# A hybrid encoder trunk: raw weight loads of the down groups first, three raw buffers, attention bias by transfers

## The chip, the cores and the metric

The kernel runs on one core of one Trainium2 chip. The metric is the device time of one execution in microseconds (us), the median of several runs.

## The reference

Four layers over a sequence of 512 tokens of width 1024, float32. Each layer is a token mixer (convolution module in layers 0 and 3, neighbourhood attention in layer 1, retention in layer 2) and a gated conv-FFN, each with a residual add. The change lies in the FFN and in attention:

```python
def conv_ffn(h, w_up, dw_w, dw_b, w_down):
    u = dwconv(h @ w_up, dw_w, dw_b)          # 1024 -> 2 * 2816, then 3 taps along the tokens
    val, gate = jnp.split(u, 2, axis=-1)
    return (jax.nn.gelu(gate) * val) @ w_down  # 2816 -> 1024

# attention, 16 heads of 64, on a grid of 8 rows x 64 columns
sc = jnp.einsum('bhqd,bhrqwd->bhqrw', q_r, k_win)
sc = sc + bias                                 # from nat_rpb, by relative row and column
p = jax.nn.softmax(sc over the 8 x 16 window)
```

## The kernel before, in words

Every product runs on TensorE in three passes over a high and a low part: a tensor is cast to its high part on ScalarE (ACT), VectorE (DVE) subtracts that from the tensor to get the low part, and `mm3` (L184 to L187) multiplies high by high, low by high, high by low. So each weight tile goes through a raw buffer (`load_raw`, tag `wr`, `NRAW` = 2 of them), a cast (`split_w`, L171) and a difference (L172) into one of three high and three low buffers.

The kernel is a program of tiles. A planner orders the instructions of each engine ahead of time from the order of the program and a timeline of its own; each engine then works through its list strictly in that order. `issue_after` (and `behind`, which looks up a noted instruction) puts an instruction behind another on the same engine's list.

The FFN walks over 22 pairs of columns, value and gate. `up(n)` makes one column of products over the normed input (24 matmuls of 512 tokens); `mid(j)` takes a pair through the three taps (L414, L416, L418), the gelu (L422) and the product (L437). Pairs of pairs make an H pair, `F`, with four blocks and three combinations of them (L444 to L447), split into `Hh` and `Hl`. The first 16 of the 22 pairs (`REST`) are multiplied down by a scheme with seven block products in place of eight, in two groups of four H pairs (`PARTS`); a group starts at the `j` in `starts` and has four macros. Each macro needs a raw weight tile (`r1`, units a11 and a22), a tile `r13` that holds the sums of two pairs of units, and a tile `sg`. `sums` fetches the latter by transfers: a plain one on SP's queue and an accumulating one on GpSimd's (POOL's) queue (L491), then the second plain one on SP's. `weights` loads the raw tile, splits it, splits `r13`, adds the raw tile to it for the third sum (L501, split into h2, l2) and makes the fourth (L505, h4, l4). `prod` multiplies: a11 and a22 first, then s2 (the third sum), s1 and s3 (`r13`), then sg and a12 for the macro before. For a group's first macro the sums are fetched before the mids of that `j`, and `weights` comes after them (`LATEW`); its products with the first three H pairs run ahead of those with the last. The wide intermediates, 128x512, are tiles `t` (`NT_FFN` = 9 buffers in the FFN).

In attention, `proj` projects q, k, v of a group of four heads; q and k are normed with squares and scaling on POOL (L907, L922) and a short chain on VectorE. `att_pair` handles two heads. For each, SP loads a table W of 384 columns (L966) and POOL adds the mask to three windows of it (L970, three adds a head, `NBM` = 2 buffers), with the adds of the first group put behind the squares. `att_step` adds the bias to the scores on VectorE (L995), ScalarE exponentiates, and so on.

Of the kernel before, what the change touches and what calls it, by code (L numbers as in the profile page):

```python
# [8 lines left out]
F32 = mybir.dt.float32  # L9
F32R = mybir.dt.float32r  # L10
# [4 lines left out]
MUL, ADD, SUB = ALU.mult, ALU.add, ALU.subtract  # L15
# [41 lines left out]
NTMP = 3  # L57
NE = 3
NO = 6
NBM = 2  # L60
NORM = "D"
NORDER = "p0 a0 p1 a1 p2 w0 a2 p3 a3 w12 w3".split()
NRAW = 2
HPO = 100000
NQZ = 2
BNG = ((0, 16, 16), (16, 28, 24), (28, 30, 30), (30, 31, 31), (31, 32, 32))
# [5 lines left out]
PART_COL = (0, 2048)  # L72
REST = 16
SLOT_H = 4
NT_FFN = 9
NWS = 3
SCALED = (5, 7, 5, 5)
UPS = ((10, 11, 18, 19), (11, 12, 18, 19), (10, 11, 18, 19), (10, 11, 18, 19))
# [9 lines left out]
def tile_trunk(  # L88
# [17 lines left out]
    def nm(s):  # L106
        uid[0] += 1
        return f"{s}{uid[0]}"
# [85 lines left out]
    def split(src, hi, lo, n=None):  # L194
        state["cast"] = nc.scalar.copy(hi, src)  # L195
        return nc.vector.tensor_tensor(lo, src, hi.bitcast(F32), SUB)  # L196
# [105 lines left out]
    def ffn(l, after):  # L302
        with ExitStack() as st:
# [101 lines left out]
            def mid(j, pv, pg):  # L405
# [41 lines left out]
                nc.vector.scalar_tensor_tensor(F[:, 6, :], F[:, 0, :], -1.0, F[:, 3, :], MUL, SUB)  # L447
                if p + 1 in (p1 for _, p1 in PARTS):
                    for c in (slice(4, 7), slice(0, 1)):
                        split(F[:, c, :], hi[:, c, :], lo[:, c, :])  # L450
                else:
                    split(F, hi, lo)
                H[p] = (hi, lo)
# [26 lines left out]
                    state["spare"] = spare  # L480
                return pss

            def sums(src, gate=None):
                n = src.shape[-1] // 4
                r13 = hp.tile([P, D], F32, tag="ws", name=nm("ws"), bufs=NWS)
                sg = hp.tile([P, D], F32, tag="wq", name=nm("wq"), bufs=2)
                with tc.issue_after(gate.ins) if gate else ExitStack():
                    nc.sync.dma_start(
                        r13[:, :2 * n].rearrange("p (b n) -> p b n", b=2),
                        src[:, 2 * n:3 * n].unsqueeze(1).broadcast_to([P, 2, n]))  # L490
                    nc.gpsimd.dma_start(r13[:, :2 * n], src[:, :2 * n], accum_op=ADD)  # L491
                    nc.sync.dma_start(sg[:, n:2 * n], src[:, 3 * n:])
                return src, r13, sg

            def weights(src, r13, sg):
                n = src.shape[-1] // 4
                r1 = load_raw(src[:, :2 * n], 2 * n)
                w1 = split_w(r1, 2 * n, nc.vector)
                w13 = split_w(r13, 2 * n, nc.vector)
                r2 = r13[:, n:2 * n]  # L500
                nc.vector.tensor_tensor(r2, r2, r1[:, :n], ADD)  # L501
                h2 = hp.tile([P, T], F32R, tag="h2", name=nm("h2"))
                l2 = hp.tile([P, T], F32R, tag="l2", name=nm("l2"))
                split(r2, h2[:, :n], l2[:, :n])
                nc.vector.tensor_tensor(sg[:, :n], r2, sg[:, n:2 * n], ADD)  # L505
                h4 = hp.tile([P, D], F32R, tag="h4", name=nm("h4"))
                l4 = hp.tile([P, D], F32R, tag="l4", name=nm("l4"))
                split(sg[:, :2 * n], h4[:, :2 * n], l4[:, :2 * n])
                u = lambda w, b: (w[0][:, b * n:(b + 1) * n], w[1][:, b * n:(b + 1) * n])
                return {"a11": u(w1, 0), "a22": u(w1, 1), "s3": u(w13, 0), "s1": u(w13, 1),  # L510
                        "s2": u((h2, l2), 0), "sg": u((h4, l4), 0), "a12": u((h4, l4), 1)}

            def down_sums(i, q, gate=None):
                p0, p1 = PARTS[q]
                c = PART_COL[q]
                return sums(f_down[l, i][:, c:c + 4 * (p1 - p0) * P], gate)

            def prod(o, w, q, b, start, stop=True, part=None):
                p0, p1 = PARTS[q]
# [110 lines left out]
            starts = {2 * p1 + (l == 1 and q == 0) * L1 + COVER[q]: q for q, (_, p1) in enumerate(PARTS)}  # L630
            for j in range(1, FT):
                ups_of(j)
                w0 = down_sums(0, starts[j], state["load"]) if j in starts else None
                if w0 and not LATEW:
                    w0 = weights(*w0)
                if n > S2[l]:
                    mids(j)
                if w0 and LATEW:
                    w0 = weights(*w0)
                if w0:  # L640
                    down(starts[j], w0, lambda: mids(j + 1), lambda: ups_of(j + 1))
            mids(FT)
# [217 lines left out]
    def nat(after):  # L860
        PER = 4
        with ExitStack() as st:
            stage_pools(st, NTMP, *NPS)
            np1 = st.enter_context(tc.tile_pool(name=nm("nat"), bufs=1, reuse_waits=RW))
            np2 = st.enter_context(tc.tile_pool(name=nm("nat2"), bufs=2, reuse_waits=RW))
            mask = np1.tile([P, 3, 256], F32, tag="mask", name=nm("mask"))
            nc.scalar.dma_start(mask, nmask.rearrange("p (v k) -> p v k", v=3))
            kstart = (0, 64, 192, 256)
            qzs = [[np1.tile([P, 2, T], F32R, tag=f"qz{n}{i}", name=nm("qz")) for i in range(2)]
                   for n in range(NQZ)]  # L870
# [24 lines left out]
            def proj(g):  # L895
                qk = np2.tile([P, 2, 4, 256], F32, tag="qk", name=nm("qk"), bufs=NQK)
                for part in range(2):
                    pss = part_proj(g, part)
                    with hp():
# [4 lines left out]
                        for t2 in range(2):  # L904
                            sqt = t512()
                            z = qk[:, part, 2 * t2:2 * t2 + 2, :]
                            state["sqt"] = nc.gpsimd.tensor_tensor(  # L907
                                sqt.rearrange("p (t d) -> p t d", t=2), z, z, MUL)
                            nc.vector.tensor_reduce(
                                ss[:, 8 * t2:8 * t2 + 8], sqt.rearrange("p (h d) -> p h d", d=HD),  # L910
                                AX.X, ADD)
# [48 lines left out]
            def att_pair(g, pi, qz, kh, kl, va, vs):  # L960
                hi = np1.tile([P, T], F32R, tag="oh", name=nm("oh"), bufs=NO)
                lo = np1.tile([P, T], F32R, tag="ol", name=nm("ol"), bufs=NO)
                bms = []
                for i2 in range(2):
                    W = np2.tile([P, 384], F32, tag="W", name=nm("W"))
                    nc.sync.dma_start(W, wd[g * PER + pi * 2 + i2])  # L966
                    bm = np1.tile([P, 3, 256], F32, tag="bm", name=nm("bm"), bufs=NBM)
                    for vi, ws in enumerate((128, 64, 0)):
                        with behind("sqt") if g == 0 else ExitStack():
                            nc.gpsimd.tensor_tensor(bm[:, vi, :], W[:, ws:ws + 256],  # L970
                                                    mask[:, vi, :], ADD)
                    bms.append(bm)
                for pr in range(2):
                    for i2 in range(2):
                        r = slice(64 * i2, 64 * i2 + 64)
                        c = slice(pr * 256, pr * 256 + 256)
                        op = att_step(g, pi, i2, pr, qz, kh, kl, bms[i2], va, vs)
                        state["att"] = split(op, hi[r, c], lo[r, c])
                return hi, lo

            def att_step(g, pi, i2, pr, qz, kh, kl, bm, va, vs):
                hh = pi * 2 + i2
# [7 lines left out]
                e = np1.tile([P, T], F32, tag="e", name=nm("e"), bufs=NE)  # L990
                mn, sx, rx = sm(2), sm(2), sm(2)
                for i in range(2):
                    vi = (0, 1, 1, 2)[pr * 2 + i]
                    ei = e[:, i * 256:(i + 1) * 256]
                    nc.vector.tensor_tensor_reduce(  # L995
                        ei, S[:, i * 256:(i + 1) * 256], bm[:, vi, :], -1.0, 3.0e38,
# [389 lines left out]
def _layout(inp):  # L1386
# [44 lines left out]
    for b, ks in ((0, 0), (1, 8), (3, 32)):  # L1431
# [2 lines left out]
        ok = (ks + kc >= start) & (ks + kc < start + 16)  # L1434
        m = np.where(ok, np.float32(0.0), np.float32(-1e30))
        masks.append(np.broadcast_to(m, (16, 8, 32, 8)).reshape(P, 256))
    nmask = np.stack(masks, 1).reshape(P, 768).astype(np.float32)
    rel = (np.arange(DTAB)[None, :] - 384 - np.arange(P)[:, None]).astype(np.float32)

    cdw = np.zeros((2, 64, 16, PH, 5, PH, 16), np.float32)  # L1440
# [71 lines left out]
```

## Time and profile before

| | us |
|---|---|
| median of 3 runs (lowest, highest) | 2544.47 (2542.74, 2549.32) |
| the profiled execution, its own time | 2544.65 |
| its span, first to last instruction | 2542.8 |
| TensorE (PE) busy | 2513.4 |
| VectorE (DVE) busy | 1832.1 |
| ScalarE (ACT) busy | 1266.9 |
| GpSimd (POOL) busy | 389.2 |

The FFNs' first products (L471) start at about 206, 826, 1620 and 2180 us; attention lies between the end of the first FFN and 826. In rows of the profile, `L171 ACT CAST wh<-wr` is a line of the kernel, an engine, an operation and what it writes and reads, with buffer numbers left out; `x` counts instructions; an arrow `<-` behind a time names what ended a wait. A line can be that of a helper, so tiles tell more than lines.

### The profile page before, as it was taken

What the parts mean: (1) busy time and instruction counts of PE and PEld (TensorE: products, weight loads), DVE (VectorE), ACT (ScalarE), POOL (GpSimd) and SP (SyncE); (2) the same over time, 40 slices, a digit from 0 to 9 for tenths busy, and PEclk for the clock granted to TensorE, in tenths of its full rate; (3) what the DMA queues carried; (4) which work ended last, traced back from release to release, by engine and by line L of the source; (5) the groups of instructions that cost most, each with busy time, mean ns of one, the idle gap of its engine ahead of it and who ended that gap; (6) DMA issues with size and microseconds to landing.
All of it is one profiled execution on the core that took longest, in us unless ns stands there. A gap on an engine that the chain in (4) does not pass through costs nothing.

```text
span 2542.8 us, 38763 instructions
## 1 busy us (share of the span) xinstructions
PE 2513.4 (99%) x15166; PEld 2171.4 (85%) x15166; DVE 1832.1 (72%) x3021; ACT 1266.9 (50%) x1778; POOL 389.2 (15%) x475
## 2 busy tenths in 40 slices
PE   9999999999999999999999999999999999999999
PEld 7878798989998889898888888889898887789897
DVE  7986767678877786767666565687677787686765
ACT  5455545465656564555332323464555445464543
POOL 1214010103421201020000000201010121111010
PEclk9999999999999999999999999999999999999999
DMA  7736766744233567673222222476674673477674
GB/s 244 234 97 180 191 154 167 172 135 121 82 92 102 145 171 160 180 185 115 83 76 74 83 75 67 141 185 161 169 169 137 203 224 92 129 195 163 166 164 141
DMA packets 123896, 370.17 MB, mean 146 GB/s; under 512 B 15120, under 2 KB 18064, under 8 KB 123712
## 3 DMA queue, kind: packets, MB, share of 16 engines
q1 hardware_dynamic: 90816, 277.30, 35.1%
q0 software_dynamic: 31600, 87.67, 18.4%
q10 hardware_dynamic: 1296, 2.72, 0.3%
q8 instruction: 119, 1.95, 0.3%
q14 instruction: 65, 0.53, 0.1%
HBM read 333.06 MB, written 30.79 MB: 143 GB/s over the span
## 4 chain that ended last, share of the span: by engine, by line
PE 88%; DVE 4%; DMA 4%; ACT 2%; issue 2%; POOL 0%; DVEq 0%; SPq 0%; ACTq 0%; POOLq 0%
PE ps L185 21%; PE ps L187 21%; PE ps L186 21%; PE ps L315 3%; PE ps L316 3%; PE ps L320 3%; DMA wr<-in_f_down 3%; PE ps L190 3%; PE ps L191 3%; PE ps L192 3%; PE ps L765 1%; DVE wl L172 1%; PE ps L764 1%; PE ps L763 1%; ACT wh L171 1%
## 5 line engine op out<-in xcount | busy, mean ns | idle before, releaser
L171 ACT CAST wh<-wr 128x1024 fp32r<-128x1024 f32 (+1 forms) x311 | 319.1, 1028 | 578.2 <-PE ps L186 280.7
L172 DVE TENSOR_TENSOR wl<-wr,wh 128x1024 fp32r<-128x1024 f32 (+1 forms) x308 | 374.4, 1216 | 197.9 <-ACT wh L171 187.6
L186 PE MATMUL ps<-xl,wh 128*128 128x512 f32 (+1 forms) x1256 | 490.0, 390 | 0.1
L185 PE MATMUL ps<-xh,wh 128*128 128x512 f32 (+1 forms) x1256 | 488.3, 390 | 0.7 <-ACT wh L171 0.7
L187 PE MATMUL ps<-xh,wl 128*128 128x512 f32 (+1 forms) x1256 | 488.6, 390 | 0.1
L185 PEld LDWEIGHTS ps<-xh,wh 128*128 128x128 f32 x1256 | 235.9, 188 | 54.4 <-ACT wh L171 1.6
L186 PEld LDWEIGHTS ps<-xl,wh 128*128 128x128 f32 x1256 | 235.9, 188 | 53.0 <-DVE xl L257 0.5
L187 PEld LDWEIGHTS ps<-xh,wl 128*128 128x128 f32 x1256 | 235.9, 188 | 52.8 <-DVE wl L172 0.5
L185 PE MATMUL ps<-Hh,wh 128*128 128x256 f32 (+1 forms) x734 | 222.5, 310 | 7.4 <-ACT Hh L195 3.7
L186 PE MATMUL ps<-Hl,wh 128*128 128x256 f32 (+1 forms) x734 | 223.8, 308 | 1.4 <-DVE Hl L196 1.4
L187 PE MATMUL ps<-Hh,wl 128*128 128x256 f32 (+1 forms) x734 | 221.9, 308 | 0.5
L315 PE MATMUL ps<-xh,wh 128*128 128x512 f32 x408 | 161.6, 396 | 0.3 <-ACT wh L179 0.3
L316 PE MATMUL ps<-xl,wh 128*128 128x512 f32 x408 | 161.1, 395 | 0.0
L190 PE MATMUL ps<-wh,xh 128*128 128x256 f32 (+1 forms) x512 | 159.0, 313 | 1.2 <-ACT xh L254 1.2
L192 PE MATMUL ps<-wh,xl 128*128 128x256 f32 (+1 forms) x512 | 159.1, 311 | 0.0
L191 PE MATMUL ps<-wl,xh 128*128 128x256 f32 (+1 forms) x512 | 158.9, 311 | 0.0
L185 PEld LDWEIGHTS ps<-Hh,wh 128*128 128x128 f32 x734 | 138.6, 190 | 19.9 <-ACT wh L171 7.3
L186 PEld LDWEIGHTS ps<-Hl,wh 128*128 128x128 f32 x734 | 138.6, 189 | 9.2 <-DVE Hl L196 1.6
L187 PEld LDWEIGHTS ps<-Hh,wl 128*128 128x128 f32 x734 | 137.8, 189 | 9.7 <-DVE wl L172 2.4
L181 POOL DMA_DIRECT2D wl<-in_f_up x51 | 45.0, 883 | 462.0 <-ACT wl L180 271.6
L185 PE MATMUL ps<-Hh,h 128*128 128x256 f32 x384 | 109.4, 285 | 0.6 <-ACT t L546 0.2
L186 PE MATMUL ps<-Hl,h 128*128 128x256 f32 x384 | 108.8, 284 | 0.0
(330 smaller groups left out, 6159.3 us busy)
## 6 DMA issues: line engine op xcount, KB each, us to landing
wr<-in_f_up SPq DMA_DIRECT2D x144, 512.0 KB, 4.1
wraw<-in_cdw SPq DMA_DIRECT2D x56, 608.0 KB, 5.0
wl<-in_f_up POOLq DMA_DIRECT2D x51, 512.0 KB, 7.8
ws<-in_f_down SPq DMA_DIRECT2D x32, 512.0 KB, 7.6
wr<-in_f_down SPq DMA_DIRECT2D x32, 512.0 KB, 7.1
ws<-in_f_down POOLq DMA_DIRECT2D x32, 512.0 KB, 8.4
xd<-t POOLq DMA_DIRECT2D x64, 256.0 KB, 6.7
wr<-in_cw_in SPq DMA_DIRECT2D x30, 512.0 KB, 4.2
```

The lines of the kernel that those rows point to most:

```text
L171: nc.scalar.copy(hi[:, :n], raw[:, :n])
L172: eng.tensor_tensor(lo[:, :n], raw[:, :n], hi[:, :n].bitcast(F32), SUB)
L181: nc.gpsimd.dma_start(lo[:, :n], src.bitcast(F32R), accum_op=ADD)
L185: nc.tensor.matmul(o, wh, ah, start=first, stop=False, skip_group_check=free)
L186: nc.tensor.matmul(o, wh, al, start=False, stop=False, skip_group_check=free)
L187: nc.tensor.matmul(o, wl, ah, start=False, stop=last, skip_group_check=free)
L190: nc.tensor.matmul(o, ah, wh, start=first, stop=False)
L191: nc.tensor.matmul(o, ah, wl, start=False, stop=False)
L192: nc.tensor.matmul(o, al, wh, start=False, stop=last)
L315: nc.tensor.matmul(ps, wh[:, s], xhi[k], start=k == 0, stop=False)
L316: nc.tensor.matmul(ps, wh[:, s], xlo[k], start=False, stop=False)
L320: nc.tensor.matmul(ps, wl[:, k * P:(k + 1) * P], xhi[k], start=False, stop=k == KD - 1)
```

## The change

- `NRAW` 2 to 3 and `NT_FFN` 9 to 7: three raw weight buffers, and in the FFN seven wide intermediates.
- A down group's first macro: its raw tile is loaded in `sums`, behind the last raw load before it, and its sums' transfers on SP come behind that load. The other macros load as before.
- In the same macro, the cast of `r13` is put behind the last Hh cast on ScalarE and its difference behind the last Hl difference on VectorE (`hold`).
- Attention bias: the mask tile, the W tiles and the adds on POOL go. `load_bias` loads the mask straight into a bias tile on SP's queue, and POOL issues a transfer from the table in memory that accumulates the three windows onto it. `NBM` 2 to 4. The masks stand in the reverse order.

```diff
-NBM = 2
+NBM = 4
-NRAW = 2
+NRAW = 3
-NT_FFN = 9
+NT_FFN = 7
...
                     for c in (slice(4, 7), slice(0, 1)):
-                        split(F[:, c, :], hi[:, c, :], lo[:, c, :])
+                        state["Hl"] = split(F[:, c, :], hi[:, c, :], lo[:, c, :])
+                        state["Hh"] = state["cast"]
...
-            def sums(src, gate=None):
+            def sums(src, gate=None, raw=False):
                 n = src.shape[-1] // 4
+                r1 = None
+                if raw:
+                    with tc.issue_after(gate.ins):
+                        r1 = load_raw(src[:, :2 * n], 2 * n)
+                    gate = state["load"]
...
-                return src, r13, sg
+                return src, r13, sg, r1
 
-            def weights(src, r13, sg):
+            def weights(src, r13, sg, r1, hold=False):
                 n = src.shape[-1] // 4
-                r1 = load_raw(src[:, :2 * n], 2 * n)
+                if r1 is None:
+                    r1 = load_raw(src[:, :2 * n], 2 * n)
                 w1 = split_w(r1, 2 * n, nc.vector)
-                w13 = split_w(r13, 2 * n, nc.vector)
+                w13 = (whi.tile([P, D], F32R, tag="wh", name=nm("wh")),
+                       wlo.tile([P, D], F32R, tag="wl", name=nm("wl")))
                 r2 = r13[:, n:2 * n]
+                with behind("Hh") if hold else ExitStack():
+                    nc.scalar.copy(w13[0][:, :2 * n], r13[:, :2 * n])
+                with behind("Hl") if hold else ExitStack():
+                    nc.vector.tensor_tensor(w13[1][:, :2 * n], r13[:, :2 * n],
+                                            w13[0][:, :2 * n].bitcast(F32), SUB)
...
-            def down_sums(i, q, gate=None):
+            def down_sums(i, q):
                 p0, p1 = PARTS[q]
                 c = PART_COL[q]
-                return sums(f_down[l, i][:, c:c + 4 * (p1 - p0) * P], gate)
+                return sums(f_down[l, i][:, c:c + 4 * (p1 - p0) * P], state["load"] if i == 0 else None, i == 0)
...
-                w0 = down_sums(0, starts[j], state["load"]) if j in starts else None
+                w0 = down_sums(0, starts[j]) if j in starts else None
...
                 if w0 and LATEW:
-                    w0 = weights(*w0)
+                    w0 = weights(*w0, True)
...
-            mask = np1.tile([P, 3, 256], F32, tag="mask", name=nm("mask"))
-            nc.scalar.dma_start(mask, nmask.rearrange("p (v k) -> p v k", v=3))
...
-                bms = []
-                for i2 in range(2):
-                    W = np2.tile([P, 384], F32, tag="W", name=nm("W"))
-                    nc.sync.dma_start(W, wd[g * PER + pi * 2 + i2])
-                    bm = np1.tile([P, 3, 256], F32, tag="bm", name=nm("bm"), bufs=NBM)
-                    for vi, ws in enumerate((128, 64, 0)):
-                        with behind("sqt") if g == 0 else ExitStack():
-                            nc.gpsimd.tensor_tensor(bm[:, vi, :], W[:, ws:ws + 256],
-                                                    mask[:, vi, :], ADD)
-                    bms.append(bm)
+                bms = [load_bias(g, pi, i2) for i2 in range(2)]
...
+            def load_bias(g, pi, i2):
+                bm = np1.tile([P, 3, 256], F32, tag="bm", name=nm("bm"), bufs=NBM)
+                w = wd[g * PER + pi * 2 + i2]
+                nc.sync.dma_start(bm, nmask.rearrange("p (v k) -> p v k", v=3))
+                nc.gpsimd.dma_start(
+                    bm, bass.AP(w.tensor, w.offset, [[384, P], [64, 3], [1, 256]]), accum_op=ADD)
+                return bm
...
-                    vi = (0, 1, 1, 2)[pr * 2 + i]
+                    vi = (2, 1, 1, 0)[pr * 2 + i]
...
-    nmask = np.stack(masks, 1).reshape(P, 768).astype(np.float32)
+    nmask = np.stack(masks[::-1], 1).reshape(P, 768).astype(np.float32)
```

More of the change, by code (lines that the diff above doesn't have):

```diff
@@ L906, in proj @@
                             z = qk[:, part, 2 * t2:2 * t2 + 2, :]
-                            state["sqt"] = nc.gpsimd.tensor_tensor(
-                                sqt.rearrange("p (t d) -> p t d", t=2), z, z, MUL)
+                            nc.gpsimd.tensor_tensor(sqt.rearrange("p (t d) -> p t d", t=2), z, z, MUL)
                             nc.vector.tensor_reduce(
```

## The prediction

> **What bounds the kernel now.** I read the page first (shares of the engines), then TensorE's waits, then the chain of waits in order of time, then TensorE's busy time in short windows around its longest waits, and last the rows of ScalarE (ACT), VectorE (DVE) and GpSimd (POOL) in those windows.
>
> ```profile
> span 2542.8 us, 38763 instructions
> ...
> PE 2513.4 (99%) x15166; PEld 2171.4 (85%) x15166; DVE 1832.1 (72%) x3021; ACT 1266.9 (50%) x1778; POOL 389.2 (15%) x475
> ```
>
> TensorE is busy for 2513.4 us of a span of 2542.8, so all its idle time together is 29.4 us. The diff adds and removes no matmul, so nothing here can bring more than those 29.4 us, the time lost at a lowered clock and small losses at the edges of waits; another engine's work matters only where TensorE waits for it. Its waits (us in total, times, longest):
>
> ```profile
> PE ps L185 <- ACT wh L171: 4.3, 8, 0.7
> PE ps L740 <- DVE t L734: 3.8, 2, 1.9
> PE ps L185 <- ACT Hh L195: 3.7, 4, 1.5
> ...
> PE ps L946 <- POOL qk L922: 1.6, 2, 1.2
> ```
>
> The first and third belong to the down groups of the FFN, which the change touches; the fourth to the start of attention, which it touches too; the second is the conv layers' and stays. The chain of waits shows what stands behind the first and third (start us, us):
>
> ```profile
> 1037.55 13.92 DMA wr<-in_f_down
> ...
> 1701.92 12.44 DMA wr<-in_f_down
> ...
> 2388.97 13.20 DMA wr<-in_f_down
> ```
>
> These are raw loads of the first macro of a down group, of which there are eight, two in each layer. The chain has six of them. A seventh, issued at 2261.77 and not in the chain, is in the list of DMA issues of that window (median us to landing last):
>
> ```profile
> wr<-in_f_down SPq DMA_DIRECT2D x1, 512.0 KB, 9.3
> ```
>
> Now TensorE around the starts of the eight groups, in time order, with one window more for its clock (second row) and one for attention (last). Columns: the window, its length, busy us (matmuls), granted clock, DMA share, GB/s.
>
> ```profile
> 308.00:316.00 8.00, 5.92 (x35) 0.81 0.35 122
> 312.00:321.00 9.00, 7.88 (x41) 0.62 0.57 154
> 440.00:448.00 8.00, 6.36 (x45) 1.00 0.32 94
> 942.00:952.00 10.00, 9.63 (x74) 1.00 0.48 114
> 1057.00:1065.00 8.00, 7.25 (x51) 1.00 0.48 161
> 1721.00:1729.00 8.00, 6.86 (x50) 1.00 0.38 119
> 1850.00:1858.00 8.00, 6.88 (x52) 1.00 0.38 121
> 2278.00:2286.00 8.00, 8.00 (x53) 1.00 0.45 142
> 2409.00:2417.00 8.00, 5.96 (x47) 1.00 0.41 118
> 606.00:614.00 8.00, 6.44 (x55) 1.00 0.45 137
> ```
>
> This is the natural experiment on which I lean. Where the load took 9.3 us (window 2278) TensorE is never idle. Where it took 12.44 us it lacks 1.14 us (window 1721), at 13.20 us 2.04 us (window 2409). The 13.92 us load costs only 0.75 (window 1057), so the relation is not strict, but the sign is plain. Why a late load hurts is seen on ScalarE in the group that starts near 1721:
>
> ```profile
> 1714.44 1.05 ACT L171 CAST wh<-wr 128x1024 fp32r<-128x1024 f32 x1 [4.94 <-DMA wr<-in_f_down]
> ...
> 1719.29 1.03 ACT L171 CAST wh<-ws 128x1024 fp32r<-128x1024 f32 x1
> ...
> 1723.82 0.62 ACT L195 CAST h<-ws 128x512 fp32r<-128x512 f32 x1 [1.06 <-DVE ws L501]
> 1724.34 0.82 ACT L195 CAST Hh<-F 128x768 fp32r<-128x768 f32 x1
> ```
>
> ScalarE stands 4.94 us for the raw weights although its next pieces of work, the activations that lead to the last H pair (Hh), do not need them: it works in order. Then the split of the sums (wh<-ws) and of the third sum (h<-ws) stand ahead of the last Hh cast, which TensorE needs first.
>
> **The change part by part.**
>
> *Raw load first, third raw buffer.* Today a raw load of the first macro can go out only when one of two buffers is free, behind the sums' five transfers on SP's queue. With three buffers it can go out in the place of the last up load, ahead of the sums. The load passes the sums' plain transfers on SP, and POOL's accumulating ones, which wait for those; they all come one 512 KB load later. They are wanted only after the last H pair, so I cost that at nothing, the cover being TensorE's up products. If that cover went, one load of 9.3 to 13.9 us would stand in the group's start. ScalarE's stand of 4.94 us and VectorE's behind it go. What is late next is the product of the last up column itself, so the H pair gains less than 4.94; but TensorE is short by only 1.14 us at 1721, a quarter of it.
>
> The terms are read as window length minus busy: 2.08 (308), 1.64 (440), 0.75 (1057), 1.14 (1721), 1.12 (1850), 2.04 (2409): 8.8 us for six starts. Window 2278 shows zero idle as what is reached when the load is in time. I take -8.8; the ends are 0 (the load is no earlier) and -8.8. The small loss at each wait's edges, while the array empties and fills, is left out.
>
> *The clock.* After the wait at 311 the granted clock is 0.62 over 312 to 321. Nine us at 0.62 lose 3.4 us of clock; TensorE is busy for 7.88 of the 9, so about 3.0 us are lost work. No other start has a clock under 1.00. I take it as a result of that wait and count -3.0; the ends are 0 and -3.0. The Trainium skill, "TensorE: Matmul & The Clock Gate", section "What's actually happening", says that the array falls to half rate after about 3.4 us of idleness, judged in a free-running window; this trace has the half rate after 2.08 us of waits inside 8, and none after 2.04 us in window 2409, so the trace differs on the length, and agrees with it in that a wait of one length may or may not bring the drop. By the page the drop need not be owed to the wait and may stay: 2536.4, the first rival below.
>
> *The sums' split behind the last combination.* For the first macro, the cast of r13 waits for the last Hh cast, its difference for the last Hl, and with them go the third sum, its split and the fourth. Behind the cast on ScalarE stands nothing that H needs; who waits is TensorE, at the products s2. VectorE's part:
>
> ```profile
> 1720.76 1.22 DVE L172 TENSOR_TENSOR wl<-ws,wh 128x1024 fp32r<-128x1024 f32 x1
> ...
> 1723.10 0.68 DVE L501 TENSOR_TENSOR ws<-ws,wr 128x512 f32<-128x512 f32 x1
> ...
> 1724.97 0.68 DVE L196 TENSOR_TENSOR l<-ws,h 128x512 fp32r<-128x512 f32 x1
> ```
>
> The moved chain is 1.03 + 1.22 + 0.68 + 0.62 + 0.68 = 4.2 us from the last H cast to the third sum's split. It is free where the last H cast ends 4.2 us before s2 starts. With ScalarE 4.94 us earlier than 1724.34 + 0.82 = 1725.16, the cast ends near 1720.2, the chain near 1724.4, and s2 starts after the 24 products that TensorE now ends about there: just covered. In exchange 1.22 + 0.68 us of VectorE's work leave the path of H. The tight case is the start at 942, whose H pair was late for VectorE's sake, not for a load's: it lacks 0.37 now; the ends are -0.4 and +4.2, and since H itself wins 1.9 there I take +0.7.
>
> *Attention bias by transfers.* Forty-eight POOL adds, sixteen W loads and one mask load from ScalarE's queue go; sixteen mask loads on SP and sixteen accumulating transfers from POOL come. (The masks' order is only turned round, at no cost.) At the start of attention POOL's six adds stand beside VectorE's short chain for the key norm:
>
> ```profile
> 601.09 4.21 POOL L970 TENSOR_TENSOR bm<-W,mask 128x256 f32<-128x256 f32 x6
> ```
>
> ```profile
> 604.66 0.67 DVE L206 TENSOR_TENSOR sm<-sm,sm 128x16 f32<-128x16 f32 x1
> 605.37 0.17 DVE L208 SCALAR_TENSOR_TENSOR sm<-sm,sm 128x16 f32<-128x16 f32 x1
> ```
>
> Steps of 0.17 us last 0.67 while POOL adds. Five of them lie in those 4.21 us, so 2.5 us go from the chain in front of POOL's scaling (L922), for which TensorE waits 1.6 us in all (waits above; window 606 lacks 1.56). I take -1.6. The new transfers' price is bounded by this row and by the spread of the bias work:
>
> ```profile
> ws<-in_f_down POOLq DMA_DIRECT2D x32, 512.0 KB, 8.4
> ```
>
> ```profile
> L970 POOL TENSOR_TENSOR bm<-W,mask x48: 723/778/1781, 601.1 to 795.6; 128x256 f32<-128x256 f32 x48
> ```
>
> Mask load and accumulation are at most two of 8.4 us, 17 us for a head pair, and eight pairs lie in 195 us, one in 24. With buffers for two pairs they come in time. What can hurt is POOL standing for a mask load with the norm's scaling behind it, and SP standing for a free bias buffer with projection loads behind it: 0 to one landing of 8.4 at the first group. I take +0.5. Its cover is that TensorE has other groups' projections; without it each of four groups could lose 8.4.
>
> *Seven intermediates.* Four wide tiles in the down groups and up to four in the mids are the demand that I count from the loops; over seven they bind for short times. No row shows a wait for a tile. The nearest is ScalarE's stand of 4.94 us above, which cost TensorE 1.14: so 0 to 1.2 at one start a layer, 0 to 5; I take +1.0. The third raw buffer elsewhere (conv, retention) I cost at nothing: TensorE's continuous work covers it.
>
> Sum: -8.8 - 3.0 + 0.7 - 1.6 + 0.5 + 1.0 = -11.2. The profiled execution took 2544.65, the median of the runs 2544.47, so they stand 0.2 apart. 2544.65 - 11.2 = 2533.4.
>
> **The rivals.**
> *The clock stays.* All goes as summed, but some wait still brings a half-rate stretch of the size in window 312: -11.2 + 3.0, 2536.4. For it: the waits of 1.9 us at VectorE (L740) stay. Against: they brought none here.
>
> *Half of it.* The load is early, but the cast of its weights waits for a split buffer (three of them) until TensorE ends the column before, and the clock still drops at some wait. For it: ScalarE waits for TensorE at most of its weight casts. Against: window 2278. Half the starts' 8.8 and attention's 1.6: 2544.65 - 6.0 = 2538.6.
>
> *No effect.* The load lands as late as before, since the same 16 engines carry the sums' transfers, and TensorE waits as now; only attention gains: 2543. Against: first on its queue, it has no sums ahead of it.
>
> *Slower.* The held split decides: at all eight starts the last H cast comes no earlier than now, and the 4.2 us chain stands open behind it. Its price is 4.2 at each start less the present waits (8.8 + 0.4): 33.6 - 9.2 = +24.4, less attention's 1.6: 2567.4. It decides from the point where more than 1.2 us a start (9.2 by 8) stands open. For it: the cover worked out above is nearly zero. With half of it open: +6.0, 2550.6. Another form is POOL standing for mask loads: 8.4 in each of four groups less the 11.7 gained without them, +21.9.
>
> The rule for POOL-issued transfers in the Trainium skill, "SBUF — State Buffer", section "Who interferes with whom", speaks for that other form: descriptors that GpSimd writes can be locked out by VectorE. The trace shows the lock between the two engines (0.67 for 0.17 us), on VectorE's side.
>
> **How the numbers follow.** Forecast 0.46 (2527 to 2537), clock stays 0.12 (2533 to 2539), half 0.20 (2536 to 2541), no effect 0.11 (2541 to 2547), slower 0.11 (over 2550). A change of 0.3%, 7.6 us, is about what a measurement of this kernel can tell from none, so faster means under 2536.8: the forecast's whole, two thirds of the clock's and a fifth of the half, 0.58; slower is over 2552.1, nearly all of its case, 0.10; the same is the rest, 0.32. Low: every gain at its end and no cost, 8.8 + 3.0 + 0.4 + 1.6 = 13.8, gives 2530.8; the uncounted edges of waits and the third buffer in other layers may add to it, so 2526. High: through no effect, 2547, which leaves out about 0.15. The forecast's own range is 2527 to 2537.
>
> **What would show it.** Right: the first raw load of a group lands before ScalarE's cast wants it, no ScalarE idle time "DMA wr<-in_f_down" at the starts, windows there with no idle time, clock 1.00 throughout, POOL's L922 wait gone. Wrong: TensorE waiting for the third sum's split (l or h) at a start; ScalarE waiting for an intermediate; POOL waiting for a mask load with L922 behind it; new waits in layers that the change does not name, since every order is planned anew.

## The result, and the profile after

| | before | after |
|---|---|---|
| median of six runs each (lowest, highest), us | 2544.64 (2542.74, 2549.32) | 2527.47 (2526.07, 2529.54) |
| profiled execution, its own time, us | 2544.65 | 2528.47 |
| its span, us | 2542.8 | 2526.7 |

The ratio is 0.993, with a 95% interval of 0.9918 to 0.9943: 17.2 us faster, where 11.2 were predicted (2533.4, range 2526 to 2547). The two profiled executions stand 16.2 apart. First the page after, engines' busy time:

```profile
span 2526.7 us, 38769 instructions
...
PE 2508.2 (99%) x15166; PEld 2170.0 (86%) x15166; DVE 1825.3 (72%) x3021; ACT 1267.8 (50%) x1778; POOL 373.0 (15%) x443
```

TensorE does the same 15166 matmuls in 5.2 us less of busy time, and its idle time fell from 29.4 to 18.5 us. Its waits after (us in total, times, longest):

```profile
PE ps L753 <- DVE t L747: 3.8, 2, 1.9
...
PE ps L185 <- ACT wh L171: 0.8, 2, 0.6
```

The first is the conv layers' wait, unchanged (L740 before). Of the 4.3 us for raw weights (wh) 0.8 are left, none of it at a group's start; the waits for `Hh` (3.7 before) and for attention's scaling (1.6) have no row any more.

To place the gain, the same stretch is read in both traces: each FFN from its first product to its last down product, and attention between the first two FFNs (window, length, busy us and matmuls, granted clock). Before:

```profile
206.69:571.63 364.94, 361.00 (x2045) 0.99 0.65 167
571.63:826.41 254.78, 250.73 (x2117) 1.00 0.36 99
826.41:1188.06 361.65, 359.86 (x2062) 1.00 0.63 160
1620.26:1980.43 360.17, 357.82 (x2044) 1.00 0.63 160
2180.05:2539.49 359.44, 357.31 (x2042) 1.00 0.64 160
```

After:

```profile
208.17:565.10 356.93, 356.93 (x2045) 1.00 0.67 170
565.10:818.19 253.09, 250.95 (x2118) 1.00 0.56 135
818.19:1175.30 357.11, 356.99 (x2062) 1.00 0.64 162
1607.49:1964.29 356.80, 356.80 (x2044) 1.00 0.64 161
2165.47:2522.90 357.43, 357.13 (x2042) 1.00 0.63 160
```

The four FFNs together took 1446.20 us and take 1428.27: 17.9 less. Length minus busy is TensorE's idle time: 10.21 us in the four FFNs before, 0.42 after. Attention is 1.7 shorter. Against that the first conv layer is 1.5 us longer (208.17 for 206.69) and the last too (2165.47 - 1964.29 = 201.2 for 199.6); the retention layer is the same, the end 0.5 longer. The sum, -17.9 - 1.7 + 1.5 + 1.6 + 0.5, is the 16.1 of the spans to within rounding.

At the starts themselves, two of the eight windows after (TensorE alone; the group's first product begins where the window does):

```profile
931.45:941.45 10.00, 10.00 (x86) 1.00 0.42 134
...
1709.18:1717.18 8.00, 8.00 (x68) 1.00 0.62 175
```

No idle time is left, as at the other six. Why, is read on SP, on the load and on ScalarE in the third FFN, the counterpart of the rows near 1714. SP's queue:

```profile
1683.18 0.33 SPq L162 DMA_DIRECT2D wr<-in_f_down  x1
1683.56 0.43 SPq L494 DMA_DIRECT2D ws<-in_f_down  x1
```

The list of DMA issues of that moment:

```profile
wr<-in_f_down SPq DMA_DIRECT2D x1, 512.0 KB, 3.9
```

ScalarE:

```profile
1695.02 1.70 ACT L195 CAST Hh<-F 128x1792 fp32r<-128x1792 f32 x1 [0.43 <-DVE F L447]
1696.63 1.04 ACT L171 CAST wh<-wr 128x1024 fp32r<-128x1024 f32 x1
```

The load goes out first, lands after 3.9 us (12.44 before), at 1687.1, and the cast at 1696.63 has no wait: the load has a margin of 9.5 us. Before, ScalarE waited for such loads 35.4 us in all, by the first row below (ScalarE's waits of the kernel before); after, it has no such row.

```profile
ACT wh L171 <- DMA wr<-in_f_down: 35.4, 7, 7.6
```

### The profile page after: what moved, and what is told of

Its sections match the earlier page's. It is cut to its first block, busy times and chain, and to the rows that moved or that the text cites. A ratio compares the mean times of both kernels' runs of the same rounds, so it can differ in the third digit from the quotient of the medians.

```text
span 2526.7 us, 38769 instructions
## 1 busy us (share of the span) xinstructions
PE 2508.2 (99%) x15166; PEld 2170.0 (86%) x15166; DVE 1825.3 (72%) x3021; ACT 1267.8 (50%) x1778; POOL 373.0 (15%) x443
## 4 chain that ended last, share of the span: by engine, by line
PE 93%; issue 3%; DVE 2%; DMA 1%; ACT 1%; SPq 0%; POOL 0%; DVEq 0%; POOLq 0%; ACTq 0%
PE ps L185 22%; PE ps L186 22%; PE ps L187 22%; PE ps L320 3%; PE ps L315 3%; PE ps L316 3%; PE ps L190 3%; PE ps L192 3%; PE ps L191 3%; PE ps L778 1%; PE ps L777 1%; PE ps L776 1%; DMA wl<-in_f_up 1%; PE ps L472 1%; PE ps L473 1%
```

## The experiments

Each kernel's profile gives the length of the four FFNs and of attention, cut as above, and the half-rate stretches of the clock in the conv layers. The times vary by some 1.5 us for each such stretch, so the lengths tell more than the medians.

| kernel | median, us | ratio to before, 95% interval | four FFNs, us | attention, us | half-rate stretches in the conv layers |
|---|---|---|---|---|---|
| before | 2543.3 to 2545.7 (by comparison) | 1 | 1446.2 | 254.8 | 0 |
| before once more | 2542.79 | 0.9983 to 1.0005 | 1442.5 | 254.9 | 2 |
| raw load first, two buffers | 2533.52 | 0.9942 to 0.9969 | 1432.0 | 254.9 | 1 |
| three buffers, seven intermediates | 2531.86 | 0.9937 to 0.9966 | 1432.4 | 254.5 | 1 |
| both | 2529.56 | 0.9926 to 0.9953 | 1429.5 | 254.3 | 3 |
| bias transfers alone | 2549.29 | 1.0009 to 1.0035 | 1449.5 | 253.5 | 3 |
| changed, no held split | 2528.51 | 0.9920 to 0.9948 | 1429.7 | 252.8 | 1 |
| changed, old bias | 2528.50 | 0.9918 to 0.9949 | 1427.9 | 254.2 | 0 |
| changed | 2527.47 | 0.9918 to 0.9943 | 1428.3 | 253.1 | 2 |
| changed once more | 2528.85 | 0.9921 to 0.9951 | 1428.5 | 253.8 | 4 |
| changed, five intermediates | 2532.09 | 0.9932 to 0.9969 | 1434.8 | 252.9 | 0 |
| before, raw weights split on GpSimd | 2533.10 | 0.9940 to 0.9967 | 1430.9 | 254.9 | 1 |
| before, raw weights loaded twice | 2550.51 | 1.0017 to 1.0042 | 1449.4 | 254.8 | 1 |
| changed, raw weights loaded twice | 2527.93 | 0.9913 to 0.9950 | 1429.0 | 253.3 | 1 |

My theory: the late raw load makes ScalarE stand, in order, ahead of the work for the last H pair; the change takes the stand away. The rivals: the third buffer alone does it, the raw weights themselves are missing, or the held split carries it.

**The raw load first, with two buffers.**

```diff
-            def sums(src, gate=None):
+            def sums(src, gate=None, raw=False):
...
+                if raw:
+                    with tc.issue_after(gate.ins):
+                        r1 = load_raw(src[:, :2 * n], 2 * n)
+                    gate = state["load"]
```

> The kernel before with one part alone: the first macro's raw load goes ahead of its sums; still two raw buffers, nine intermediates, no held split, the old attention bias. Theory (order): the load was late because the sums' five transfers stood ahead of it; alone on its queue it lands 4 us after issue in place of 7 to 14, ScalarE's idle time for it at the starts goes, and most of the FFN's part of the 17.2 us comes: 2544.6 - 13 = 2531.6, and 2535 at most if the wait for one of two buffers gives some back. Rival (buffer): with two buffers the load cannot go out before a buffer is free, SP stands for it with the sums queued behind, and the time stays at 2542 to 2547. Rival (sums late): TensorE waits at the starts for the third sum's split (l or h), slower than 2547.

2533.52 came (the theory had 2531.6 to 2535). The load takes 3.8 us with two buffers as well; the list of DMA issues near 1694 and ScalarE's cast (two views of this kernel):

```profile
wr<-in_f_down SPq DMA_DIRECT2D x1, 512.0 KB, 3.8
```

```profile
1701.52 1.04 ACT L171 CAST wh<-wr 128x1024 fp32r<-128x1024 f32 x1
```

No wait stands behind the cast. SP's row shows when the load went out:

```profile
1694.05 0.33 SPq L162 DMA_DIRECT2D wr<-in_f_down  x1
```

Counted from this FFN's start (1612.38; 1620.26 before) that is 81.7 us, as in the kernel before (1701.92): with two buffers the load leaves no earlier. It lands 8.6 us sooner (3.8 for 12.44) because nothing stands ahead of it. What two buffers keep is a loss in the second FFN (360.7 us, for 357.1 in the changed kernel). Its first start, the window that was 942 to 952, has the very row of before, 9.63 busy and 74 matmuls, with the load early, so the load does not cause that loss:

```profile
935.08:945.08 10.00, 9.63 (x74) 1.00 0.47 119
```

**Three buffers, the load behind its sums.**

```diff
-NRAW = 2
+NRAW = 3
-NT_FFN = 9
+NT_FFN = 7
```

> The kernel before with three raw buffers and seven intermediates alone; the first macro's raw load still stands behind its sums. Theory (order): the load still lands 9 to 14 us after issue, so the starts gain little: 2540 to 2545. Rival (buffer): the load goes out earlier by the third buffer, and that alone brings 10 us or more: 2534 or less. If seven intermediates cost anything, as I had it with 1.0 us, it shows here as a ScalarE wait for a tile t and as time above 2545.

Here the theory of the order was wrong: 2531.86, almost as much as by the order. The load is still slow, but goes out earlier (SP's queue, DMA issues, ScalarE):

```profile
1687.92 0.33 SPq L162 DMA_DIRECT2D wr<-in_f_down  x1
```

```profile
wr<-in_f_down SPq DMA_DIRECT2D x1, 512.0 KB, 10.2
```

```profile
1701.37 1.04 ACT L171 CAST wh<-wr 128x1024 fp32r<-128x1024 f32 x1
```

Counted from the FFN's start (1611.55 here, 1620.26 before), the issue is at 76.4 us in place of 81.7 (1701.92), the landing at 86.6 in place of 94.1, the cast at 89.8. So a 10.2 us load is harmless when it lands 3.2 us ahead of the cast. The two parts of the change are two ways to the same thing, and each alone is enough for most of it.

**Both, without the held split and the new bias.** The two edits above together.

> The kernel before with three raw buffers, seven intermediates and the raw load first; no held split, the old attention bias. Theory: all of the gain but attention's 1.7 us and what the held split brings: 2527.5 + 1.7 = 2529.2, or up to 2531 with some 0.2 us a start for the third sum's work ahead of the last H pair. Rival (held split): the sums' split ahead of the last combination costs TensorE its 1.03 + 0.62 us on ScalarE at each of eight starts, 2536 or more, with waits for Hh at the starts in the profile.

2529.56 (2529.2 expected), the FFNs at 1429.5: 2.5 and 2.9 us less than with either part alone. The rival is out.

**The late load without the in-order stand.** In the kernel before, with the load where it was, the first macro's raw weights are cast and subtracted on GpSimd:

```diff
-                w1 = split_w(r1, 2 * n, nc.vector)
+                if pool:
+                    w1 = (whi.tile([P, D], F32R, tag="wh", name=nm("wh")),
+                          wlo.tile([P, D], F32R, tag="wl", name=nm("wl")))
+                    nc.gpsimd.tensor_copy(w1[0][:, :2 * n], r1[:, :2 * n])
+                    nc.gpsimd.tensor_tensor(w1[1][:, :2 * n], r1[:, :2 * n],
+                                            w1[0][:, :2 * n].bitcast(F32), SUB)
+                else:
+                    w1 = split_w(r1, 2 * n, nc.vector)
```

`pool` is set for a group's first macro.

> The kernel before, with only the first macro's raw weights cast and subtracted on GpSimd in place of ScalarE and VectorE; the load goes out where it did, with two buffers. It takes the in-order stand away and leaves the load as late as it was. Theory (the stand is what costs): the load still takes 9 to 14 us and lands as before, ScalarE has no idle time for it, the last H pair is in time, and most of the 14 us of the starts go: 2530 to 2536. GpSimd's difference takes 2.4 us where VectorE's takes 1.2, so a wait for the raw weights themselves may keep 1 us at some starts. Rival (the late weights themselves): TensorE waits for wh or wl of the first products as long as it waited for H, and the time stays at 2541 to 2547.

2533.10. The load is as late as before (DMA issues near 1694), GpSimd stands for it, ScalarE goes on, TensorE is never idle at that start (GpSimd's rows, ScalarE's, TensorE's window):

```profile
wr<-in_f_down SPq DMA_DIRECT2D x1, 512.0 KB, 12.6
```

```profile
1707.16 1.44 POOL L501 CAST wh<-wr 128x1024 fp32r<-128x1024 f32 x1 [1.89 <-DMA wr<-in_f_down]
1708.68 2.73 POOL L502 TENSOR_TENSOR wl<-wr,wh 128x1024 fp32r<-128x1024 f32 x1
```

```profile
1706.35 0.63 ACT L422 ACTIVATE t<-t 128x512 f32<-128x512 f32 x1 [2.14 <-DVE t L418]
```

```profile
1714.43:1722.43 8.00, 8.00 (x68) 1.00 0.51 163
```

This separates the stand from the lateness: the same late load costs nothing when the work ahead of H does not queue behind it. The four FFNs take 1430.9 us with no early load at all. The edit also takes the cast (1.05 us) and the difference off ScalarE and VectorE, so alone it would leave open whether that work was the cost; with the raw load first and two buffers both stay where they were, and the four FFNs take 1432.0 us.

**The raw weights loaded twice, in the kernel before.**

```diff
                 r1 = load_raw(src[:, :2 * n], 2 * n)
+                if twice:
+                    state["load"] = nc.sync.dma_start(r1[:, :2 * n], src[:, :2 * n])
```

`twice` is set for a group's first macro.

> The kernel before, with the first macro's raw weights loaded twice into the same buffer, one load behind the other: the second lands some 4 to 9 us later than the one load did. Theory (a stand of ScalarE is free up to about 3 us and costs TensorE one for one beyond): eight starts are each 4 to 9 us later, less at the one with slack: +30 to +65 us, 2575 to 2610, and per start TensorE's loss is ScalarE's idle time less 3 us. Rival (the starts are bound by something else, the load only coincides): +10 or less, 2555 or less.

2550.51: the theory's number failed, and the rival's holds (+6.7 us). The rows say why, and it is not the rival's reason. ScalarE's rows at the start that was at 1721 (the second load left at 1716.98), and TensorE's window:

```profile
1716.08 0.63 ACT L422 ACTIVATE t<-t 128x512 f32<-128x512 f32 x1 [2.13 <-DVE t L418]
1717.47 0.84 ACT L195 CAST Hh<-F 128x768 fp32r<-128x768 f32 x1 [0.76 <-DVE F L437]
1722.63 1.06 ACT L171 CAST wh<-wr 128x1024 fp32r<-128x1024 f32 x1 [4.33 <-DMA wr<-in_f_down]
```

```profile
1723.00:1731.00 8.00, 7.73 (x56) 1.00 0.19 65
```

The planner knew of both loads and put the gelu and the first part of the last H pair ahead of the cast. The raw weights come 6 us later in this FFN than before (1722.63 - 1622.47 = 100.2 from its start, for 1714.44 - 1620.26 = 94.2), ScalarE stands 4.33 us, and TensorE lacks 0.27 us where it lacked 1.14. So my price, one for one beyond a slack, holds only for the order in which it was read; what counts is what stands behind the cast in ScalarE's list. Most of what was lost lies in the second FFN (367.1 us, for 361.7 before), with two half-rate stretches; there TensorE waits for the late weights themselves, 1.1 us at its first start (wl) and 1.9 at its second (wh).

**The raw weights loaded twice, in the changed kernel.** The same edit in `sums`, with the sums' transfers behind both loads.

> The changed kernel with the same doubling: the first macro's raw weights loaded twice, the sums' transfers behind both. Theory: the load lands 9 us ahead of ScalarE's cast, so a second load of 4 us more is hidden, and the sums, 4 to 8 us later, are wanted only after the last H pair: 2527 to 2531. Rival (the sums have no cover): TensorE waits for the sums' split (h, l or wh<-ws) at the starts, 2540 or more.

2527.93. SP's queue and ScalarE: the second load goes out when the first has landed, the sums 5 us later than without it, and the cast has no wait.

```profile
1684.11 0.33 SPq L162 DMA_DIRECT2D wr<-in_f_down  x1
1688.33 0.33 SPq L490 DMA_DIRECT2D wr<-in_f_down  x1
1688.71 0.44 SPq L495 DMA_DIRECT2D ws<-in_f_down  x1
```

```profile
1697.55 1.05 ACT L171 CAST wh<-wr 128x1024 fp32r<-128x1024 f32 x1
```

The sums do have the cover that I gave them, at least for 5 us.

**The kernel before once more.** No edit.

> The kernel before once more. Theory: its first raw loads land anew, each somewhere between 7 and 15 us after its issue, so the loss at each start differs from the first profile by ScalarE's idle time, one for one beyond 3 us; the time lies between 2539 and 2551, a wider spread than the changed kernel's 2526 to 2532. Rival: the landings repeat within 0.5 us, and the spread of the times has another cause.

One landing moved. In one and the same program the first load of the last group took 13.2 us in the first profile and 8.3 in this one; the other seven first loads came within 0.75 us of the first profile, so the rival's "the landings repeat" is nearer the truth for them. ScalarE's row and TensorE's window here:

```profile
2399.41 1.06 ACT L171 CAST wh<-wr 128x1024 fp32r<-128x1024 f32 x1 [0.78 <-DMA wr<-in_f_down]
```

```profile
2410.00:2418.00 8.00, 8.00 (x65) 1.00 0.50 165
```

In the first profile ScalarE stood 5.70 us there. That row and the casts at four other starts show what a stand costs (ScalarE of the kernel before):

```profile
434.45 1.05 ACT L171 CAST wh<-wr 128x1024 fp32r<-128x1024 f32 x1 [5.42 <-DMA wr<-in_f_down]
1051.55 1.05 ACT L171 CAST wh<-wr 128x1024 fp32r<-128x1024 f32 x1 [5.14 <-DMA wr<-in_f_down]
1843.12 1.05 ACT L171 CAST wh<-wr 128x1024 fp32r<-128x1024 f32 x1 [4.76 <-DMA wr<-in_f_down]
2271.18 1.05 ACT L171 CAST wh<-wr 128x1024 fp32r<-128x1024 f32 x1 [1.83 <-DMA wr<-in_f_down]
2402.24 1.05 ACT L171 CAST wh<-wr 128x1024 fp32r<-128x1024 f32 x1 [5.70 <-DMA wr<-in_f_down]
```

Set beside TensorE's idle time in the windows that the prediction shows: 5.42 gave 1.64, 4.94 gave 1.14, 4.76 gave 1.12, 5.70 gave 2.04; 1.83, and 0.78 in the second profile, gave nothing. The differences are 3.78, 3.80, 3.64 and 3.66: a stand of 3.7 us is free, and beyond it TensorE's idle time grows one for one. (The expectations say 3 us, since they count the edges of the waits as loss.) The second profile bears it out at three of the same starts: 5.45 gave 1.68, 5.18 gave 1.38 and 4.86 gave 1.22, so 3.77, 3.80 and 3.64 were free. The free part belongs to the order at a start and is no constant. The second FFN has another plan: 5.14 gave 0.75 at its second start, so 4.4 were free. At the first FFN's first start, the largest stand of all, 7.58, gave only 2.08, and in the second profile 6.87 gave 1.58, so 5.5 and 5.3 were free. The kernel before lay between 2538.81 and 2550.61 in the runs of the first comparison; the changed kernel, between 2526.07 and 2532.65 in all of its own.

**The bias transfers alone, in the kernel before.** The change's `load_bias`, `NBM` and masks, with the FFN as before.

> The kernel before with the attention bias by transfers alone; the FFN as before. Theory: the wait for the scaling at attention's start (1.6 us in the waits) goes and nothing else, 2544.6 - 1.7 = 2542.9; attention's stage is 1.7 us shorter in the profile and the other stages are the same within 0.3 us, but for half-rate stretches. Rival: the transfers cost as much as they bring, 2544.6 or more. Rival (planner): the orders of other layers move and bring or cost several us.

2549.29: slower, by 6 us. Attention is 1.3 us shorter, as expected, so the loss lies elsewhere. Outside attention, every engine's list and SP's are those of the kernel before. But the loads landed later in this profile (eight stands of ScalarE for 43.3 us in its waits, seven for 35.4 before), above all at the start that was free:

```profile
2278.20 1.05 ACT L171 CAST wh<-wr 128x1024 fp32r<-128x1024 f32 x1 [6.29 <-DMA wr<-in_f_down]
```

The last FFN takes 363.7 us for 359.4, and the two conv layers 4.8 more with three half-rate stretches. That accounts for this profile; why the landings and the clock came out worse in most of its twelve runs is open.

**The changed kernel without the held split.**

```diff
-                    w0 = weights(*w0, True)
+                    w0 = weights(*w0)
```

> The changed kernel without the held split: the first macro's sums are split where the order has them, and all else is as changed. Theory (a start has some 3 us of slack for ScalarE, as the starts of the kernel before show, where 1.83 us of standing cost nothing and 4.76 us cost 1.7): the hold is worth little, 2527 to 2529. Rival (my +0.7): the hold costs, and without it the time falls to 2526.8 or less. Rival (the hold carries it): 2531 or more, with waits for Hh at the starts.

**The changed kernel with the old bias.** The FFN as changed, attention as before.

> The changed kernel with the old attention bias (mask tile, W tiles, adds on GpSimd). Theory: 1.3 to 1.7 us more than the changed kernel, 2529; attention's wait for the scaling is back at 1.6 us, and the other stages are the same within 0.3 us but for half-rate stretches. Rival (the bias alone, put into the kernel before, came out slower by 6 us, so it may cost here too): without it the time falls, 2525 or less.

**The changed kernel once more.** No edit.

> The changed kernel once more, as the base of its two neighbours on this chip: 2527.5 within 1.5 us. Theory of the clock: its half-rate stretches come where TensorE has waited 1.9 us or more, which are now the two waits of the conv layers, and may fall at one, both or neither of them; each costs about 1.5 us. Rival: the stretches lie at fixed places and the same two are seen again.

The three medians, 2528.51, 2528.50 and 2528.85, are the same within the spread of the runs. The lengths tell more. With the held split the four FFNs take 1427.9 to 1428.5 in three profiles (1429.0 with the doubled load), without it 1429.5 and 1429.7: it brings about 1.2 us, nearly all in the second FFN (358.2 without it, 356.8 to 357.2 with it). With the transfers attention takes 252.8 to 253.8 us in six profiles, with the adds 254.2 to 254.9: 1.4 us on the mean. The wait is back with the old bias (TensorE's waits of that kernel):

```profile
PE ps L959 <- POOL qk L935: 1.5, 2, 1.2
```

Both are smaller than what the medians can tell, and shown in the lengths alone. The expectation on the clock held in part: of the four half-rate stretches in this profile of the changed kernel two follow the waits of 1.9 us, the other two follow pairs of waits of 0.9 us (the last section has the reason).

**Five intermediates.**

```diff
-NT_FFN = 7
+NT_FFN = 5
```

> The changed kernel with five wide intermediates in the FFN in place of seven. Theory: the demand stays at six or fewer for nearly all of the time, so seven cost nothing (I had counted 1.0), and five begin to bind: ScalarE or VectorE waits for a tile t in the mids, which costs TensorE 0 to 8 us, 2527 to 2536. Rival: seven bind already, and five cost much more, 2540 or more.

2532.09, the FFNs at 1434.8, 6.4 us more. ScalarE waits for a tile t until its transfer into the running sum in memory (`xd`) has let it go; with seven this row does not exist:

```profile
ACT t L559 <- DMA xd<-t: 30.0, 7, 5.0
```

## Why the prediction was right, and where its terms were off

The sign, the place and the mechanism came as argued: the load lands before the cast wants it, ScalarE's stand is gone, the windows at the starts have no idle time, L922's wait is gone, and no new wait of more than 0.3 us came at TensorE. One sign did not come: the clock is not 1.00 throughout. That the time lies inside the range is in part luck. With every gain at its end the sum reached 2530.8, and 2527.47 lies below that; it is covered only by the 4.8 us that were added, without a working, for the edges of waits and the third buffer. These two did bring something, but their size was a guess. The terms were off as follows.

- **The starts, -8.8.** The idle time came nearly whole: 9.8 us went from the FFNs. Mis-sized was what I left out, the edges of the waits. In the third FFN, where the clock is full in both, 2.35 us of idle time went and the stage is 3.37 shorter (360.17 to 356.80): half a microsecond for each of two starts. Over the four FFNs the edges and the clock make 17.9 - 9.8 = 8.1 us; less the 3.0 of the clock, 5.1. This is the larger part of the error, but not all of it is half a microsecond a start: 2.9 of it lies in the second FFN (4.54 us shorter for 1.67 us of idle time), and the held split's 1.2 is a part of that. There the window 942 to 952, read as 0.37 us short, holds 74 matmuls, and its counterpart after holds 86.
- **The relation that "is not strict".** I set the load's duration beside TensorE's loss. The right column was ScalarE's stand, which gives 3.7 us free and one for one beyond at four starts, with more free at the starts that have another order. "The H pair gains less than 4.94; TensorE is short by a quarter" was that slack, unread.
- **The clock, -3.0.** The stretch behind 311 went, with its loss. But two half-rate stretches came in the conv layers, 1.5 us each, so that the term is 0 in this profile. This is what the rival "the clock stays" named: the conv waits of 1.9 us. The reading of the first stretch was off as well: the half rate began at 313.0, between the two waits, so 1.42 us of waiting came ahead of it and not 2.08.
- **The held split, +0.7.** Wrong in sign: about -1.2, in the second FFN, the tight case I had named. The products covered the 4.2 us chain; that VectorE's work left the path of H is the likely reason for the gain, and was not tried by itself.
- **Attention, -1.6.** 1.4 on the mean of the lengths, 1.7 in the two profiles. The new transfers' +0.5 is in that number and cannot be seen by itself; POOL does stand for mask loads, 72.2 us in its waits, but TensorE has no wait for POOL any more.
- **Seven intermediates, +1.0.** No wait for a tile with seven; with five, 6.4 us. The limit lies below seven; six was not run.
- **The third buffer, "0 elsewhere"**, and its part at the starts: I took it as the means to send the load first. With seven intermediates and no other edit it brings most of the gain by itself (2531.86).

Where half a microsecond hides is seen in TensorE's rows at the start near 2409, before:

```profile
2411.39 0.28 PE L187 MATMUL ps<-Hh,wl 128*128 128x256 f32 x1
2413.15 0.38 PE L185 MATMUL ps<-Hh,wh 128*128 128x256 f32 x1 [1.48 <-ACT Hh L195]
2414.10 0.38 PE L185 MATMUL ps<-Hh,wh 128*128 128x256 f32 x1 [0.56 <-ACT wh L171]
```

In the stream ahead of these rows the matmuls start 0.12 us apart, though each is shown as 0.28 us of busy time. At the two waits the starts lie 1.76 and 0.95 us apart, and 0.22 to the one after; less three steps of 0.12 that is 2.57 us lost, where the idle time shows 2.04.

The rival "no effect" said that the same 16 engines carry the sums and the load lands as late: against it, 3.9 us.

## What to carry to other kernels

A load that an in-order engine waits for is not priced by its duration or by its lateness, but by what stands behind the waiting instruction in that engine's list: the same load, 12.6 us long, cost nothing when another engine stood for it. Read the stand of the waiting engine, find the slack up to which it is free, and count the edges of its waits (half a microsecond a start here) beside the idle time. Behind that slack lies the next limit: with the doubled load TensorE waited up to 1.9 us for the weights themselves. Where a load lands close to a limit, two profiles of one program are the cheapest experiment there is.

## What the hardware showed beyond that

Whether a short wait brings the half rate depends on where it falls. In the first and the last conv layer of one trace (raw load first, two buffers) TensorE has the same wait of 1.92 us. Its windows, laid out in steps of 3.41 us from the start of that trace's half-rate stretch at 2095.33:

```profile
129.25:132.66 3.41, 2.46 (x11) 1.00 0.79 238
132.66:136.08 3.42, 2.45 (x38) 1.00 0.32 97
...
2091.92:2095.33 3.41, 1.49 (x13) 1.00 0.08 34
2095.33:2098.74 3.41, 3.41 (x36) 0.50 0.57 127
2098.74:2102.15 3.41, 3.41 (x60) 1.00 0.43 126
```

The first wait is split between two windows, 0.95 and 0.97 us, and the clock stays. The second lies in one window, and the next window runs at half rate: the busy time is full, but 36 matmuls go through for 60. In the fourteen traces the stretches of one trace start whole multiples of 3.413 us apart, the one behind each program's last product counted; in the second profile of the changed kernel they start at 134.94, 148.59, 2094.19 and 2107.84, which is 4, 570 and 4 steps. Laid out so, all 17 windows inside the programs, behind the first 20 us, with 1.92 to 2.05 us of idle time were followed by a stretch, of 22 windows with 1.41 to 1.84 us eight were, and below that none was, but for the second half of the one long stretch. What decides between 1.41 and 1.84 us is open. The steps lie elsewhere in every run, so the stretches come and go: one and the same program had two of them in the conv layers in one profile and four in another.

Each such stretch lasted 3.4 us (6.8 once, at the first start in the first profile) and cost about 1.5: the first conv layer takes 206.7 to 207.4 us without one, 208.2 to 208.9 with one, 209.7 and 210.0 with two. The Trainium skill, "TensorE: Matmul & The Clock Gate", section "What's actually happening", has a window of 3.4 us that runs freely and drops the rate after an idle one. The stretches' length and their fixed steps agree with it; the idle time does not, since a window with 1.92 of its 3.41 us idle was enough here.
